# Splitting weight chunks with two GpSimd DMAs and a ScalarE negation instead of a ScalarE cast and a VectorE subtraction

## The chip, the cores and the metric

The kernel runs on one core of a Trainium2 chip. The metric is device time in microseconds (us) of one execution. The engines are PE (TensorE matmul, with PEld for its weight loads), DVE (VectorE), ACT (ScalarE), POOL (GpSimd) and SP (SyncE, which here only issues DMAs). A change of less than 0.2% of the time (1.8 us) counts below as no change, since the three runs of before differ by about that much.

## What is computed

One block of a hybrid network in fp32, for 512 tokens of width 1024:

```python
h = rms_norm(x, norm1_g)
u_x, u_g, q, k, v, g_r, g_a = split(h @ w_in)
y_rnn  = rg_lru(causal_depthwise_conv(u_x), ...) * gelu(u_g)
y_attn = diff_attention(rope(q), rope(k), v, ...)
merged = sigmoid(g_r) * (y_rnn @ w_br_rnn) + sigmoid(g_a) * (y_attn @ w_br_attn)
x  = x + merged @ w_out
x  = x + square(relu(rms_norm(x, norm2_g) @ w_mlp1)) @ w_mlp2
out = rms_norm(x, normf_g)
```

## The kernel before

Every large product is made of three fp32r matmuls, so that fp32 accuracy is kept: both operands are split into a high part rounded to fp32r and a low part that is the remainder, and `mm` adds high x high, high x low and low x high in one PSUM bank (lines 168, 169 and 170).

The weights come in chunks of 128 x 1024 fp32 (512 KB, one block of 128 output columns over all 1024 rows). `chunk_plan` lists them in the order of use: chunks 0 to 7 are V, chunks 8 to 39 are Q, K, U_X and U_G (head by head, with the attention and the recurrent unit beside them), chunks 40 to 71 are the gates and the two branch projections, chunks 72 to 79 are `w_out`. The MLP that follows has its own path (`make_piece`, `hold`) and its own ring.

Two chunks are loaded by one 1 MB DMA on SP into a `raw` tile (two buffers). `emit_chunk` then splits one chunk in two instructions: ACT casts the raw values into the high tile (line 137), DVE subtracts the high tile from the raw values into the low tile (line 138). `wslot` says where they go: tiles `whi` and `wlo` with four buffers each, and for every fifth chunk of the first 40 the tiles `E0` and `E1`. `chunk(c)` emits the split of chunk c+4 (c+3 from about chunk 36 on) before it hands out chunk c, so a split can start when the matmuls of an earlier chunk have released its buffer. A chunk is consumed by `proj`: 24 matmuls of 512 columns. The result in PSUM (tag `mm`, three buffers) is taken away by ACT or DVE; in the merge stage ACT applies the sigmoid to a gate's result and DVE multiplies it with the branch's result.

Each engine runs its own queue in order. A scheduler decides at build time where each instruction stands in its engine's queue; it is not written out by hand. An instruction whose input or buffer isn't ready holds up everything behind it on its engine.

Of the kernel before, what the change touches and what calls it, by code (L numbers as in the profile page):

```python
# [8 lines left out]
F = mybir.dt.float32  # L9
FR = mybir.dt.float32r  # L10
AF = mybir.ActivationFunctionType
ALU = mybir.AluOpType
AX = mybir.AxisListType

P = 128
T = 512
D = 1024
KT = D // P
# [75 lines left out]
class Build:  # L94
# [19 lines left out]

    def emit_chunk(self, c, parts=False):
        nc = self.nc
        if c // 2 not in self.raw:
            raw = self.t("raw", (P, 2, D), bufs=2)
            if c < 4:
                for j in range(4):  # L120
                    nc.sync.dma_start(self.x_in[2 * c + j], self.a["xT"][2 * c + j])
                    nc.sync.dma_start(
                        raw[:, j // 2, (j % 2) * T:(j % 2 + 1) * T],
                        self.a["wts"][c // 2, :, j * T:(j + 1) * T],
                    )
            else:
                nc.sync.dma_start(raw.rearrange("p c f -> p (c f)"), self.a["wts"][c // 2])
            self.raw[c // 2] = raw
        raw = self.raw[c // 2][:, c % 2]
        th, tl, bufs = self.wslot(c)  # L130
        hi = self.t(th, (P, KT, P), FR, bufs=bufs)
        lo = self.t(tl, (P, KT, P), FR, bufs=bufs)
        hf, lf = hi.rearrange("p k m -> p (k m)"), lo.rearrange("p k m -> p (k m)")
        self.split[c] = (hi, lo)

        def part(s):
            nc.scalar.copy(hf[:, s], raw[:, s])  # L137
            nc.vector.tensor_tensor(lf[:, s], raw[:, s], hf[:, s].bitcast(F), op=ALU.subtract)  # L138

        if parts:  # L140
            return part
        part(slice(0, D))
# [827 lines left out]
```

## Time and profile before

| what | us |
|---|---|
| median of three runs | 894.05 (892.45 to 894.46) |
| the profiled execution's own time | 893.03 |
| its span, first to last instruction | 891.2 |
| PE busy in the span | 879.4 |
| DVE busy | 582.0 |
| ACT busy | 474.3 |
| POOL busy | 0.3 |

The span is the stretch that the profile shows; the time of the execution is 1.8 us longer. The engines work side by side, so their busy times don't add up. POOL does five small fills and issues no DMA; all loads and stores are issued by SP.

### The profile page before, as it was taken

The page shows a single profiled execution, that of the slowest core. Times are in us where ns is not written, and L with a number is a line of the kernel's source. Part 1 is how long each engine was busy: PE and PEld are TensorE (multiplying, and loading weights), DVE is VectorE, ACT ScalarE, POOL GpSimd, SP SyncE. Part 2 cuts the span into 40 slices and gives each one's busy share as a digit, 9 for nine tenths or more (in the row PEclk, how much of TensorE's full clock was granted, in tenths as well). Part 3 has the DMA queues.
Part 4 walks back from the last instruction along what each step waited for, and adds up shares of the span by engine and source line. Part 5 has one row for each costly group of instructions (what it writes and reads, how often), then busy time and mean ns, then how long its engine had stood idle before and what let it go on. Part 6 is the DMA issues. An engine that isn't in the chain of part 4 may idle for free.

```text
span 891.2 us, 12316 instructions
## 1 busy us (share of the span) xinstructions
PE 879.4 (99%) x4817; PEld 737.9 (83%) x4817; DVE 582.0 (65%) x995; ACT 474.3 (53%) x857; POOL 0.3 (0%) x5
## 2 busy tenths in 40 slices
PE   9999999999999999999999999999999999999996
PEld 7887778777777788888888889888888888888996
DVE  7777688787887756333333897776666666666633
ACT  7644777957867983322222456655444444445532
POOL 0000000000000000000000000000000000000000
PEclk9999999999999999999999999999999999999998
DMA  8443123132223022222522222232222223322211
GB/s 290 146 143 118 60 71 130 51 121 78 71 105 120 3 95 95 95 94 95 177 95 93 69 102 82 79 112 95 95 96 95 98 101 108 113 92 106 95 49 48
DMA packets 20746, 88.60 MB, mean 99 GB/s; under 512 B 3024, under 2 KB 6352, under 8 KB 11728
## 3 DMA queue, kind: packets, MB, share of 16 engines
q1 hardware_dynamic: 20688, 87.81, 28.7%
q8 instruction: 38, 0.62, 0.3%
q14 instruction: 20, 0.16, 0.1%
HBM read 81.51 MB, written 2.10 MB: 94 GB/s over the span
## 4 chain that ended last, share of the span: by engine, by line
PE 96%; DMA 1%; DVE 1%; ACT 1%; issue 0%; SPq 0%; DVEq 0%; ACTq 0%
PE pmm L242 22%; PE pmm L168 16%; PE pmm L170 15%; PE pmm L169 15%; PE psc L242 15%; PE psc L410 2%; PE psc L498 2%; PE pmm L410 2%; PE pmm L533 2%; PE ptr L521 1%; DMA raw<-wts 1%; PE psc L594 1%; DMA L<-xT 1%; PE ptr L341 0%; PE psc L596 0%
## 5 line engine op out<-in xcount | busy, mean ns | idle before, releaser
L197 ACT CAST whi<-raw 128x512 fp32r<-128x512 f32 (+1 forms) x144 | 87.9, 630 | 134.4 <-PE pmm L242 56.7
L137 ACT CAST whi<-raw 128x1024 fp32r<-128x1024 f32 (+1 forms) x76 | 76.3, 1006 | 134.4 <-PE pmm L169 125.0
L168 PE MATMUL pmm<-X,whi 128*128 128x512 f32 x328 | 132.4, 404 | 0.0
L169 PE MATMUL pmm<-X,whi 128*128 128x512 f32 x328 | 130.1, 397 | 0.0
L170 PE MATMUL pmm<-X,wlo 128*128 128x512 f32 x328 | 130.0, 396 | 0.0
L138 DVE TENSOR_TENSOR wlo<-raw,whi 128x1024 fp32r<-128x1024 f32 (+1 forms) x76 | 88.4, 1164 | 60.2 <-ACT whi L137 59.6
L198 DVE TENSOR_TENSOR wlo<-raw,whi 128x512 fp32r<-128x512 f32 (+1 forms) x144 | 100.0, 703 | 34.2 <-ACT whi L197 31.8
L242 PE MATMUL psc<-X,whi 128*128 128x256 f32 x448 | 84.1, 286 | 0.6 <-DVE up L816 0.2
L168 PEld LDWEIGHTS pmm<-X,whi 128*128 128x128 f32 x328 | 61.7, 188 | 18.1 <-issue 2.6
L170 PEld LDWEIGHTS pmm<-X,wlo 128*128 128x128 f32 x328 | 61.7, 188 | 15.0
L242 PEld LDWEIGHTS psc<-X,whi 128*128 128x128 f32 x448 | 69.0, 188 | 5.9 <-DVE up L816 1.7
L169 PEld LDWEIGHTS pmm<-X,whi 128*128 128x128 f32 x328 | 61.8, 188 | 14.3 <-issue 0.4
L242 PE MATMUL psc<-X,wlo 128*128 128x256 f32 x224 | 60.8, 280 | 0.0
L302 ACT ACTIVATE B<-psc,nb 128x128 f32<-128x128 f32 (+3 forms) x64 | 33.2, 523 | 26.9 <-DVE nb L503 23.9
L242 PE MATMUL psc<-L,whi 128*128 128x256 f32 x224 | 43.7, 291 | 1.7 <-DVE tmp L812 1.7
L302 ACT ACT_TABLE_LOAD x32 | 41.1, 1283 | 1.1 <-DVE nb L503 0.5
L242 PEld LDWEIGHTS psc<-X,wlo 128*128 128x128 f32 x224 | 41.3, 188 | 0.0
L242 PE MATMUL pmm<-R,whi 128*128 128x512 f32 x128 | 41.1, 392 | 0.0
L242 PEld LDWEIGHTS psc<-L,whi 128*128 128x128 f32 x224 | 34.3, 188 | 7.4 <-DVE tmp L812 4.3
L242 PE MATMUL pmm<-Q,whi 128*128 128x512 f32 x128 | 39.7, 391 | 0.0
L242 PE MATMUL pmm<-B,whi 128*128 128x256 f32 (+1 forms) x160 | 37.5, 325 | 0.0
L242 PE MATMUL pmm<-V,whi 128*128 128x512 f32 (+1 forms) x128 | 32.4, 338 | 0.0
(318 smaller groups left out, 1886.3 us busy)
## 6 DMA issues: line engine op xcount, KB each, us to landing
raw<-wts SPq DMA_DIRECT2D x70, 1024.0 KB, 4.8
rot<-B SPq DMA_DIRECT2D x64, 64.0 KB, 2.0
L<-xT SPq DMA_DIRECT2D x8, 256.0 KB, 5.4
raw<-wts SPq DMA_DIRECT2D x8, 256.0 KB, 5.4
E<-xT SPq DMA_DIRECT2D x8, 256.0 KB, 4.8
out<-E SPq DMA_DIRECT2D x6, 256.0 KB, 3.2
tmp<-gates SPq DMA_DIRECT2D x8, 128.0 KB, 4.7
out<-E SPq DMA_DIRECT2D x4, 128.0 KB, 2.8
```

The lines of the kernel that those rows point to most:

```text
L137: nc.scalar.copy(hf[:, s], raw[:, s])
L138: nc.vector.tensor_tensor(lf[:, s], raw[:, s], hf[:, s].bitcast(F), op=ALU.subtract)
L168: nc.tensor.matmul(ps, hi[:, k], xh[k], start=(k == 0), stop=False)
L169: nc.tensor.matmul(ps, hi[:, k], xl[k], start=False, stop=False)
L170: nc.tensor.matmul(ps, lo[:, k], xh[k], start=False, stop=(k == KT - 1))
L197: self.nc.scalar.copy(hi, src)
L198: self.nc.vector.tensor_tensor(lo, src, hi.bitcast(F), op=ALU.subtract)
L242: nc.tensor.matmul(out, l[:, k], r, start=((first if clear is None else clear) and k == 0 and g == 0), stop=(last and k == 3 and g == 2), ...
L302: ins = A.activation(*args, **kw).ins
L410: TE.matmul(pvs[half][i], xs[q][:, i * P:(i + 1) * P], (hv, lv)[wi][:, q % 2], start=(q == 0 and n == 0), stop=(q == KT - 1 and n == 2))
L498: TE.matmul(sc[:, m, :n], l[rows, 0, i * P:n], r[rows, 1, :n], start=(g == 0), stop=(g == 2))
L533: TE.matmul(po[:, i], pdT[:, j], v[j][:, h * P:(h + 1) * P], start=(j == 0), stop=(j == i))
```

## The change

For every chunk from 8 on, `emit_chunk` leaves SP's raw load, ACT's cast and DVE's subtraction out. The high tile is written by a DMA that GpSimd issues straight from the weights in HBM and that casts fp32 to fp32r. ACT then writes the negated high part into the low tile, and a second GpSimd DMA adds the raw weights from HBM onto that tile. Chunks 0 to 7 and the MLP weights stay as they were.

```diff
     def emit_chunk(self, c, parts=False):
         nc = self.nc
+        if c >= 8:
+
+            src = self.a["wts"][c // 2, :, c % 2 * D:(c % 2 + 1) * D]
+            th, tl, bufs = self.wslot(c)
+            hi = self.t(th, (P, KT, P), FR, bufs=bufs)
+            lo = self.t(tl, (P, KT, P), FR, bufs=bufs)
+            hf, lf = hi.rearrange("p k m -> p (k m)"), lo.rearrange("p k m -> p (k m)")
+            nc.gpsimd.dma_start(hf, src)
+            nc.scalar.mul(lf, hf.bitcast(F), -1.0)
+            nc.gpsimd.dma_start(lf, src, accum_op=ALU.add)
+            self.split[c] = (hi, lo)
+            return
         if c // 2 not in self.raw:
```

This is POOL's queue in the middle of the merge stage after the change; before, POOL's queue holds no DMA anywhere. L124 is the casting DMA of a chunk and L126 its accumulating DMA; `whi_666` and `wlo_667` are the two tiles of one chunk, `whi_669` and `wlo_670` those of the next, and so on.

```order
L124 DMA whi_666_3258<-wts 128x1024
L126 DMA wlo_667_3259<-wts 128x1024
L124 DMA whi_669_3289<-wts 128x1024
L126 DMA wlo_670_3290<-wts 128x1024
L124 DMA whi_674_3325<-wts 128x1024
L126 DMA wlo_675_3326<-wts 128x1024
L124 DMA whi_677_3356<-wts 128x1024
L124 DMA whi_681_3388<-wts 128x1024
L126 DMA wlo_678_3357<-wts 128x1024
L126 DMA wlo_682_3389<-wts 128x1024
```

The first three chunks stand one by one: the cast of a chunk is queued behind the accumulation of the chunk before. The last two stand as a pair, with both casts ahead of both accumulations. From chunk 48 to chunk 53 six chunks stand one by one; then seven times a pair and a single; then a single, a pair and two singles. The four chunks 44 to 47 ahead of them overlap. Of chunks 8 to 43, 24 stand one by one and 12 as six pairs.

ACT's queue at the same place before the change. L302 is the sigmoid of a gate's result in PSUM, L137 the cast of a chunk, L353 the high part of the merged result:

```order
L302 ACTIVATE tmp_687_3258<-pmm_690_3263 128x512
L137 CAST whi_697_3326<-raw_691_3289 128x1024
L353 CAST R0_695_3322<-tmp_687_3258 128x512
L137 CAST whi_701_3358<-raw_700_3356 128x1024
L302 ACTIVATE up2_696_3325<-pmm_699_3330 128x512
L137 CAST whi_705_3389<-raw_700_3356 128x1024
L137 CAST whi_709_3421<-raw_708_3419 128x1024
L302 ACTIVATE tmp_704_3388<-pmm_707_3393 128x512
```

And after it (the same three lines are now L314, L125 and L365; the buffer numbers are others):

```order
L125 ACTIVATE wlo_670_3290<-whi_669_3289 128x1024
L365 CAST R0_672_3321<-tmp_665_3257 128x512
L125 ACTIVATE wlo_675_3326<-whi_674_3325 128x1024
L314 ACTIVATE up2_673_3324<-pmm_676_3330 128x512
L125 ACTIVATE wlo_678_3357<-whi_677_3356 128x1024
L125 ACTIVATE wlo_682_3389<-whi_681_3388 128x1024
L314 ACTIVATE tmp_680_3387<-pmm_683_3393 128x512
```

In this piece each cast has become a negation at the same place to within one instruction. The negation waits for a DMA where the cast waited for a buffer that PE releases, and the sigmoids and casts behind it wait with it.

## Rows read from the trace of the kernel before

**Rows 1.** The page, parts 1 and 2: busy time of engines, tenths in 40 slices.

```profile
PE 879.4 (99%) x4817; PEld 737.9 (83%) x4817; DVE 582.0 (65%) x995; ACT 474.3 (53%) x857; POOL 0.3 (0%) x5
...
PE   9999999999999999999999999999999999999996
```

**Rows 2.** Stretches: length, busy time of engines, PE clock, DMA share, GB/s.

```profile
29.00:52.70 23.70, 23.70 (x112) 19.43 (x110) 18.02 (x40) 13.08 (x20) 0.00 (x0) 1.00 0.38 130
52.70:321.70 269.00, 268.96 (x1312) 209.81 (x1310) 207.98 (x382) 192.54 (x376) 0.00 (x0) 1.00 0.26 86
321.70:529.00 207.30, 207.30 (x925) 168.48 (x925) 102.33 (x138) 73.95 (x114) 0.00 (x0) 1.00 0.29 102
529.00:825.00 296.00, 293.72 (x1914) 262.69 (x1913) 204.29 (x344) 149.15 (x273) 0.00 (x0) 1.00 0.28 97
```

**Rows 3.** The page, part 4: the chain that ended last, by engine.

```profile
PE 96%; DMA 1%; DVE 1%; ACT 1%; issue 0%; SPq 0%; DVEq 0%; ACTq 0%
```

**Rows 4.** ACT's timeline: start, length, what, idle time before and its releaser.

```profile
400.10 1.05 ACT L137 CAST whi<-raw 128x1024 fp32r<-128x1024 f32 x1 [4.27 <-PE pmm L169]
401.06 0.59 ACT L302 ACTIVATE tmp<-pmm 128x512 f32<-128x512 f32 x1
405.62 1.05 ACT L137 CAST whi<-raw 128x1024 fp32r<-128x1024 f32 x1 [3.97 <-PE pmm L169]
...
422.51 1.05 ACT L137 CAST whi<-raw 128x1024 fp32r<-128x1024 f32 x1 [4.56 <-PE pmm L169]
```

**Rows 5.** Groups by line and shape: count, busy us, mean ns, idle before.

```profile
L138 DVE TENSOR_TENSOR wlo<-raw,whi 128x1024 fp32r<-128x1024 f32 x68 | 82.9, 1221 | 59.9 <-ACT whi L137 59.3
L197 ACT CAST whi<-raw 128x512 fp32r<-128x512 f32 x140 | 83.9, 618 | 132.4 <-PE pmm L242 56.7 <-PE psc L242 48.1 <-DVE raw L214 15.9
L319 ACT ACTIVATE X<-L,small 128x512 fp32r<-128x512 f32 x15 | 10.6, 717 | 5.5 <-PE pmm L410 4.0 <-DMA L<-xT 1.5
```

**Rows 6.** DMA: the queue's total, then issues with size and us to landing.

```profile
q1 hardware_dynamic: 20688, 87.81, 28.7%
...
raw<-wts SPq DMA_DIRECT2D x70, 1024.0 KB, 4.8
rot<-B SPq DMA_DIRECT2D x64, 64.0 KB, 2.0
```

**Rows 7.** SP's timeline: one issue of a 1 MB load.

```profile
161.82 0.33 SPq L127 DMA_DIRECT2D raw<-wts  x1
```

**Rows 8.** ACT's line 137 from 52.7 to 321.7 us: what ended its waits.

```profile
  PE pmm L169: 26.6, 10
```

## The prediction

> **What bounds the kernel now.** I read the engines' busy shares first, then the stretches, then the chain. PE is busy 879.4 of 891.2 us [rows 1], and the chain that ended last is PE for 96% [rows 3]. The stretches sharpen this [rows 2]. The chunks that the change touches run from 52.7 to 529 us, and PE's idle time there is 0.04 us. DVE is busy 208 of 269 us in the first part and 102 of 207 in the second, so it has room; ACT has 76 us of room in the first part and 133 in the second. Removing work from DVE or ACT can therefore give back next to nothing. What counts is whether a chunk's two tiles still arrive before PE wants them.
>
> In the merge stage PE takes 5.60 us a chunk: four successive casts span 400.10 to 422.51 us [rows 4]. Chunks 44 to 79 take 207.3/36 = 5.8 us on average and chunks 8 to 43 take 269/36 = 7.5 us, the attention's matmuls included [rows 2]. ACT's casts wait for PE to release a buffer, up to 4.56 us, and start as soon as it does [rows 4]. The lead is large: with four buffers a released one is needed again three chunks later, 3 x 5.60 = 16.8 us, and cast plus subtraction fill it in 1.05 + 1.22 us [rows 4, 5].
>
> **The change part by part.** Removed: 72 subtractions of 1.22 us on DVE (88 us [rows 5]), worth nothing in time, since PE's work covers them; 36 loads of 1 MB on SP, hidden as well. ACT's 72 casts of 1.05 us become 72 negations. A scaled copy on half the columns takes 0.717 against 0.618 us for a cast [rows 5], so I take 1.15 us; the 7 us in all lie in ACT's room. The transfers change from 72 x 512 KB read once to read twice, and the second one also reads and rewrites the low tile.
>
> What costs is the new chain of a chunk: POOL issues the cast, it lands, ACT negates, POOL issues the accumulation, it lands. POOL runs in order, so where chunks stand one by one, the next cast can't be issued before this chunk's negation. That gives POOL a cycle time of its own. None of these DMAs is in the trace, so I bound them.
>
> Transfer: 64 KB land in 2.0 us and 1 MB in 4.8 [rows 6], a line of 1.8 us plus 2.9 us per MB. 512 KB alone lands in 3.3 us; that is the lower end. The accumulation moves its bytes over at least two reads, so I count it as 1 MB. It is issued right ahead of the next cast and the two share the 16 DMA engines; sharing evenly, the cast has landed when 1 MB has moved, 4.7 us, and the accumulation when 1.5 MB has, 6.2 us. The upper end is half that speed, for casting or adding on the way: 7.6 and 10.6 us. I take 4.7 and 6.2, since the nearest row, the 1 MB load, moves as much through the same engines.
>
> Issue on POOL: SP spends 0.33 us on a load [rows 7]; that is the lower end. The upper end is 2.0 us, the whole of the shortest DMA [rows 6]. I take 1.0 us. ACT: 1.15 us for the negation and 0.25 for the semaphores and a short queue, 1.4 us; the sigmoid ahead of it would add 0.59 [rows 4].
>
> The cast then costs 1.0 + 4.7 = 5.7 us to landing. A single takes 5.7 + 1.4 + 1.0 = 8.1 us of POOL's cycle; a pair, whose second negation follows the first, 5.7 + 2 x 1.4 + 1.0 = 9.5 us. The whole chain of one chunk is 5.7 + 1.4 + 1.0 + 6.2 = 14.3 us of the 16.8, so 2.5 us of slack.
>
> Chunks 8 to 43: 24 singles and six pairs need 24 x 8.1 + 6 x 9.5 = 251 us, and PE takes 269, so weights keep up on the whole. ACT pays instead: ten casts waited for a buffer there, 26.6 us [rows 8], and those ten will wait for the cast's landing as well, 10 x 5.7 = 57 us more. ACT's room is 269 - 192.5 - 26.6 = 50 us beyond these waits [rows 2, 8]. What is behind it on ACT is the softmax and the recurrent unit's sigmoids, for which PE waits. I charge the excess, **7 us**; ends 0 (the buffered PSUM tiles cover it) and 57.
>
> Chunks 44 to 79: the first four overlap and cost nothing. Six singles lag by 6 x (8.1 - 5.6) = 15.0 us. A pair and a single take 17.6 us against PE's 16.8, seven times 0.8 = 5.6. The last five take 3 x 8.1 + 9.5 = 33.8 against 28.0, 5.8. Together 26.4, less the slack of 2.5: **24 us**. Behind the late negations stand the sigmoids and with them DVE's multiplications; three PSUM buffers give these two chunks of time, so they add nothing of their own.
>
> Sum: 893.0 (the profiled execution, 1 us under the median of the runs shown) + 24 + 7 = **924 us**.
>
> A rule speaks against this result. The Trainium skill, "DMA: Bandwidth & Descriptors", section "Anatomy of one DMA — SWDGE (gpsimd) path", gives a DMA from GpSimd about 2.0 us fixed plus its bytes at 436 GB/s; for 512 KB that is an estimate of 3.2 us, near the line's 3.3 us, and with it alone the sum would stay at 893 (the first rival's place). The line from SP's loads agrees with it to 0.1 us; no row of before shows a DMA from GpSimd.
>
> **The rivals.** *Hidden after all: 893.* At the lower ends the cast lands in 0.33 + 3.3 = 3.6 us, a single cycles in 3.6 + 1.4 + 0.33 = 5.3 us, under PE's 5.6, the chain takes 3.6 + 1.4 + 0.33 + 3.3 = 8.6 of 16.8 us, and ACT's ten waits grow by 36 us, under its 50. For it speaks that the DMA engines are loaded to 28.7% only [rows 6]; against it, that every term must stay near its lower end, since six singles in a row, with the 8.2 us of slack that this chain leaves, allow a cycle of 7.0 us at most. This is the case that isn't slower.
>
> *Slow transfers: about 1,063.* At half speed the cast lands in 8.6 us; a single is 11.0, a pair 12.4. Chunks 44 to 79 lag by 6 x 5.4 + 7 x 6.6 + 17.4 = 96 us, and by 4.8 more since the chain is 21.6 us long, over the 16.8; chunks 8 to 43 need 24 x 11.0 + 6 x 12.4 = 338 us against 269, 69 more. 893 + 101 + 69 = 1,063. The engines themselves speak for it: 87.81 MB took 28.7% of 891.2 us [rows 6], 1.53 us per 512 KB; a cast and a double-sized accumulation at half speed would take 9.2 us of them a chunk, more than PE's 5.6 or 7.5. At full speed they take 4.6, which fits. If only POOL's issue is at its upper 2.0 us, a single takes 10.1 us and a pair 11.5: 311 us against 269 in the first part, 74 us of lag in the second, about 1,010.
>
> *POOL held up by DVE: about 950.* If POOL's descriptor work has to wait while DVE holds a port, an issue waits on average half of a 1.22 us operation in the share of time that DVE is busy: 0.77 in the first part, 0.49 in the second [rows 2, 5], 0.5 and 0.3 us an issue, two issues a chunk. Singles become 9.1 and 8.7 us. The first part then needs 24 x 9.1 + 6 x 10.5 = 281 us, 12 over; in the second the lags grow by 14. The Trainium skill, "SBUF — State Buffer", section "SBUF: two separate sides", has this lock for DVE's two-port modes; no run here shows it yet.
>
> *Faster: about 891.* The raw tiles come free earlier for the MLP; PE's idle time from 529 to 825 us is 2.3 us [rows 2], and all of it would have to vanish.
>
> **How the numbers follow.** My own case, weights late by a few us in the merge stage: 0.40, with its own range of 897 to 960. Held up by DVE, inside that range: 0.05. Hidden: 0.20. Slow transfers or a slow issue, 960 to 1,100: 0.27; beyond: 0.05. Faster: 0.03. The range of 892 to 1,070 leaves out the faster case and the upper half of the slow one with what lies beyond, about 0.2. The bound for no change is 0.2%, or 1.8 us. Faster 0.03, same 0.20, slower 0.77.
>
> **What the profile would show.** Right: PE idle from some 350 us on, ended by the DMA into `wlo`, some 24 us in all and almost none before 321 us; POOL's queue alternating with a period near 8 us for singles; cast DMAs landing in 4 to 6 us, accumulations in 5 to 7; ACT's idle time before line 125 ended by the cast DMA; DVE's busy time near 494 us. Wrong: no PE idle time there (hidden); DMA engines near full with landings of 8 us and more (slow transfers); long issues on POOL (slow issue). What would make it wrong most easily is the price of an accumulating DMA, the term that rests on the farthest row, or ACT's waits stopping PE in the attention stage, where I charge only 7 us.

## The result and the profile after

The changed kernel takes 1000.1 us (median of three runs, 998.0 to 1002.68) against 894.05: 1.119 times the time before (95% interval 1.117 to 1.121). The forecast was 924 us in a range of 892 to 1,070. The direction and the range held; the move was 106 us where 30 were expected.

The page after, parts 1 to 3, answers to [rows 1, 6]: busy times, the tenths of PE and of its granted clock in 40 slices, and the two DMA queues (q0 is GpSimd's).

```profile
PE 907.4 (91%) x4817; PEld 752.9 (75%) x4817; DVE 499.3 (50%) x923; ACT 472.8 (47%) x857; POOL 103.3 (10%) x149
...
PE   8996798799799599899888988899999999999996
...
PEclk9997899799799799999999999999999999999998
...
q0 software_dynamic: 20736, 75.51, 33.2%
q1 hardware_dynamic: 15504, 50.06, 14.9%
```

PE has gaps from the fourth slice on, through both stages, and its busy time has grown by 28 us for the same 4817 instructions, with a granted clock of 0.7 to 0.8 in the slices in which PE is busy for 5 to 7 tenths. DVE has lost 83 us of work, and it bought nothing.

The two stages as stretches, with the columns of [rows 2]:

```profile
55.00:384.90 329.90, 284.71 (x1312) 220.07 (x1310) 165.81 (x330) 192.65 (x376) 50.52 (x71) 0.92 0.56 127
384.90:632.00 247.10, 217.44 (x927) 171.94 (x926) 60.89 (x101) 73.29 (x112) 47.53 (x66) 0.97 0.66 155
```

The attention stage has grown from 269.0 to 329.9 us, the merge stage from 207.3 to 247.1. The span grew by 109.6: 2.3 ahead of the stages, 60.9, 39.8, and 6.6 behind them. Within the attention stage PE's busy time rose by 15.7 us and its idle time to 45.2; within the merge stage by 10.1 and to 29.7. PE's waits in the attention stage, 55.0 to 384.9 us (who waits, for whom: us in all, times, the longest):

```profile
PE psc L606 <- ACT L L314: 28.6, 4, 11.4
PE psc L507 <- DVE B L489: 8.8, 1, 8.8
PE psc L606 <- ACT gwh L601: 7.4, 2, 3.8
```

And in the merge stage:

```profile
PE pmm L182 <- DMA wlo<-wts: 21.1, 11, 3.0
PE ptr L574 <- DVE V L332: 5.5, 2, 3.9
PE pmm L180 <- ACT Q L365: 2.9, 1, 2.9
PE pmm L181 <- DVE Q L366: 0.2, 1, 0.2
```

These rows add up to the idle time, 44.8 of 45.2 and 29.7 of 29.7 us. In the merge stage PE waits for weights, as forecast. In the attention stage no row names a weight: PE waits for the recurrent unit's gates (lines 601 to 608) and once for the rotated Q and K (line 489), all from ACT and DVE. ACT's own waits for casts in that stage are 22, with 87.9 us (L125 is the negation; `E` stands for the tiles `E0` and `E1`):

```profile
ACT wlo L125 <- DMA whi<-wts: 72.5, 18, 8.7
ACT E L125 <- DMA E<-wts: 15.4, 4, 6.9
```

The waits of POOL, ACT and DVE over the whole span, in this order:

```profile
POOL wlo L126 <- ACT wlo L125: 337.1, 58, 11.7
POOL whi L124 <- PE pmm L182: 60.3, 19, 7.9
...
ACT wlo L125 <- DMA whi<-wts: 185.9, 39, 9.2
...
DVE B L487 <- DMA rot<-B: 62.5, 13, 16.8
```

The DMA issues with their size and median us to landing:

```profile
whi<-wts POOLq DMA_DIRECT2D x65, 512.0 KB, 6.9
wlo<-wts POOLq DMA_DIRECT2D x65, 512.0 KB, 5.5
...
rot<-B SPq DMA_DIRECT2D x64, 64.0 KB, 5.5
```

POOL stands 337 us behind negations and ACT 186 us behind casts (the tiles `E0` and `E1` add 33 and 17). The prediction hadn't looked at the last row: the 64 KB loads of the rotary embedding, issued by SP and untouched by the diff, take 5.5 us instead of 2.0 [rows 6], and DVE waits 62.5 us for them (3.9 before). Not all of this is the landing: the loads start from ACT's copies of Q and K (line 478), and these stand behind negations as well. Two such copies at 64.06 and 74.33 us, for example, stand behind negations that had waited 5.22 and 8.73 us for their casts; DVE then waits 16.77 and 6.79 us for the loads.

POOL's timeline in the merge stage shows its cycle:

```profile
434.34 0.86 POOL L126 DMA_DIRECT2D wlo<-wts  x1 [6.63 <-ACT wlo L125]
434.88 0.89 POOL L124 DMA_DIRECT2D whi<-wts  x1
443.10 0.86 POOL L126 DMA_DIRECT2D wlo<-wts  x1 [7.33 <-ACT wlo L125]
443.64 1.43 POOL L124 DMA_DIRECT2D whi<-wts  x2
451.43 0.89 POOL L126 DMA_DIRECT2D wlo<-wts  x1 [6.36 <-ACT wlo L125]
452.74 0.87 POOL L126 DMA_DIRECT2D wlo<-wts  x1 [0.41 <-ACT wlo L125]
453.54 0.62 POOL L124 DMA_DIRECT2D whi<-wts  x1
462.16 0.87 POOL L126 DMA_DIRECT2D wlo<-wts  x1 [8.00 <-ACT wlo L125]
```

A single takes 8.76 us (434.34 to 443.10), a pair and a single 19.06 (443.10 to 462.16). PE can use a chunk every 5.60.

How a late cast reaches PE in the attention stage is seen near 250 us and near 340 us, first on ACT's timeline:

```profile
250.05 1.06 ACT L125 ACTIVATE wlo<-whi 128x1024 fp32r<-128x1024 f32 x1 [3.56 <-DMA whi<-wts]
251.01 0.39 ACT L601 CAST gwh<-tmp 128x256 fp32r<-128x256 f32 x1
...
336.91 1.06 ACT L125 ACTIVATE wlo<-whi 128x1024 fp32r<-128x1024 f32 x1 [7.70 <-DMA whi<-wts]
```

And on PE's:

```profile
251.45 0.80 PE L606 MATMUL psc<-L,gwh 128*128 128x512 f32 x1 [3.68 <-ACT gwh L601]
252.05 0.63 PE L607 MATMUL psc<-R,gwh 128*128 128x512 f32 x1
...
257.55 0.39 PE L180 MATMUL pmm<-X,whi 128*128 128x512 f32 x1
...
342.05 0.80 PE L606 MATMUL psc<-L,gwh 128*128 128x512 f32 x1 [11.38 <-ACT L L314]
```

ACT stands 3.56 us in front of a negation whose cast hasn't landed. The gate's cast, whose input SP had loaded from 225.28 us on, is next in ACT's queue, and PE waits 3.68 us for it. The last two lines are the longest wait of the stage: ACT stands 7.70 us in front of a negation, the softmax and a gate's sigmoid (line 314) come behind it, and PE waits 11.38 us. Of PE's seven waits in this stage five, with 30.8 us, have such a stand of ACT at a negation (3.3 to 7.7 us) right ahead. The other two, 8.8 us until 86.27 and 5.3 us until 111.82, follow waits of DVE for rotary loads. After the wait near 250 us the same 512 columns take 0.63 us, later 0.39: the granted clock is 0.50 from 251.40 to 256.70, the lower of the two levels (1.2 of 2.4 GHz). Such stretches are where the added busy time comes from: the mean granted clock is 0.92 in the attention stage and 0.97 in the merge stage, against 1.00 before, so a wait here costs more than its length.

### The profile page after: what moved, and what is told of

Its sections match the earlier page's. It is cut to its first block, busy times and chain, and to the rows that moved or that the text cites. A ratio compares the mean times of both kernels' runs of the same rounds, so it can differ in the third digit from the quotient of the medians.

```text
span 1000.8 us, 12512 instructions
## 1 busy us (share of the span) xinstructions
PE 907.4 (91%) x4817; PEld 752.9 (75%) x4817; DVE 499.3 (50%) x923; ACT 472.8 (47%) x857; POOL 103.3 (10%) x149
## 3 DMA queue, kind: packets, MB, share of 16 engines
q0 software_dynamic: 20736, 75.51, 33.2%
HBM read 119.26 MB, written 2.10 MB: 121 GB/s over the span
## 4 chain that ended last, share of the span: by engine, by line
PE 55%; issue 20%; DMA 14%; POOL 4%; ACT 3%; DVE 3%; SPq 0%; POOLq 0%; DVEq 0%; ACTq 0%
PE pmm L254 19%; PE psc L254 13%; DMA whi<-wts 8%; PE pmm L182 5%; PE pmm L180 5%; PE pmm L181 5%; DMA wlo<-wts 2%; POOL whi L124 2%; PE pmm L422 2%; PE psc L422 2%; POOL wlo L126 1%; DMA raw<-wts 1%; PE psc L510 1%; ACT wlo L125 1%; DMA E<-wts 1%
## 5 line engine op out<-in xcount | busy, mean ns | idle before, releaser
L125 ACT ACTIVATE wlo<-whi 128x1024 fp32r<-128x1024 f32 x65 | 68.8, 1058 | 229.4 <-DMA whi<-wts 185.9
L209 ACT CAST whi<-raw 128x512 fp32r<-128x512 f32 (+1 forms) x144 | 87.9, 630 | 126.3 <-PE pmm L254 56.9
L182 PE MATMUL pmm<-X,wlo 128*128 128x512 f32 x328 | 133.4, 407 | 7.5 <-DMA wlo<-wts 7.5
L180 PE MATMUL pmm<-X,whi 128*128 128x512 f32 x328 | 135.7, 414 | 0.0
L181 PE MATMUL pmm<-X,whi 128*128 128x512 f32 x328 | 132.6, 404 | 0.0
L126 POOL DMA_DIRECT2D wlo<-wts x65 | 56.6, 870 | 376.6 <-ACT wlo L125 337.1
L182 PEld LDWEIGHTS pmm<-X,wlo 128*128 128x128 f32 x328 | 63.9, 195 | 24.8 <-DMA wlo<-wts 9.2
L180 PEld LDWEIGHTS pmm<-X,whi 128*128 128x128 f32 x328 | 63.8, 194 | 18.8 <-issue 2.3
L181 PEld LDWEIGHTS pmm<-X,whi 128*128 128x128 f32 x328 | 63.7, 194 | 14.6
L124 POOL DMA_DIRECT2D whi<-wts x65 | 47.4, 760 | 98.6 <-PE pmm L182 60.3
L705 DVE TENSOR_TENSOR tmp<-pmm,tmp 128x512 f32<-128x512 f32 x8 | 5.5, 691 | 76.2 <-PE pmm L182 51.0
L606 PE MATMUL psc<-L,gwh 128*128 128x512 f32 x16 | 10.3, 643 | 36.4 <-ACT L L314 28.6
L487 DVE TENSOR_TENSOR B<-B,up 128x512 f32<-128x512 f32 x16 | 11.0, 691 | 62.5 <-DMA rot<-B 62.5
```

Source lines behind the costliest of these rows:

```text
L124: nc.gpsimd.dma_start(hf, src)
L125: nc.scalar.mul(lf, hf.bitcast(F), -1.0)
L126: nc.gpsimd.dma_start(lf, src, accum_op=ALU.add)
L180: nc.tensor.matmul(ps, hi[:, k], xh[k], start=(k == 0), stop=False)
L181: nc.tensor.matmul(ps, hi[:, k], xl[k], start=False, stop=False)
L182: nc.tensor.matmul(ps, lo[:, k], xh[k], start=False, stop=(k == KT - 1))
```

## The experiments

Three theories. **A**: ACT's queue, held up at negations behind a cast's landing, is the cause. **B**: POOL's cycle is, since its in-order queue puts cast, negation and accumulation of successive chunks one behind the other. **C**: the crowded DMA engines are, since they make the casts and the rotary loads late. This table has the stages of the profiled executions and the times in us. The ratios are to runs of before on the same chip, made beside each kernel. The attention stage runs from the first projection with chunk 8 to the first projection with chunk 44, a branch projection; the merge stage runs from there to the end of `w_out`.

| kernel | attention stage | merge stage | median | ratio to before (95%) |
|---|---|---|---|---|
| before | 269.0 | 207.4 | 894.05 | |
| after | 329.9 | 247.1 | 1000.1 | 1.117 to 1.121 |
| e1 negation on POOL | 360.5 | 355.5 | 1133.6 | 1.267 to 1.271 |
| e2 no accumulation | 280.3 | 209.9 | 906.6 | 1.011 to 1.018 |
| e3 high part only | 288.5 | 208.8 | 921.1 | 1.029 to 1.033 |
| e4 merge stage only | 268.9 | 245.3 | 938.8 | 1.048 to 1.054 |
| e5 cast one chunk ahead | 290.9 | 211.3 | 922.3 | 1.031 to 1.036 |
| e6 low part only | 292.1 | 208.2 | 917.9 | 1.023 to 1.030 |
| e7 plain loads, twice | 273.0 | 207.5 | 898.7 | 1.003 to 1.007 |
| e8 negation on DVE | 335.8 | 263.2 | 1026.2 | 1.145 to 1.155 |
| e9 = e5 without rotary loads | 274.7 | 211.8 | 905.0 | 1.011 to 1.014 |
| e10 = after without rotary loads | 312.8 | 243.7 | 973.2 | 1.084 to 1.090 |
| e11 = before without rotary loads | 270.3 | 207.6 | 896.5 | 1.002 to 1.004 |
| e12 = e4 with the cast one ahead | 269.0 | 209.6 | 898.4 | 1.003 to 1.006 |

**e1 and e8: the negation on another engine.** On POOL, ACT has no part in the split; on DVE, a faster engine does it.

```diff
-            nc.scalar.mul(lf, hf.bitcast(F), -1.0)
+            nc.gpsimd.tensor_scalar(lf, hf.bitcast(F), -1.0, None, op0=ALU.mult)   # e1
+            nc.vector.tensor_scalar(lf, hf.bitcast(F), -1.0, None, op0=ALU.mult)   # e8
```

> The negation moves from ACT's queue to POOL's own queue; both DMAs stay. Theory A (ACT is held up: in the attention stage ACT's softmax, sigmoids and gate casts stand behind negations that wait for the cast to land, and PE waits for them): the attention stage, 330 us in the changed kernel and 269 before, comes back to under 290 us, and PE's waits for ACT at the recurrent gates (36 us) go to under 8. Theory B (POOL's cycle: weights are late because cast, negation and accumulation follow each other on POOL): the merge stage (247 us against 207) stays above 240 and may grow, since a cycle of 6.9 + negation + 0.9 us remains, and the attention stage comes back little, to over 315. Theory C (the DMA engines are crowded, so the rotary loads and the casts land late): nothing comes back in the attention stage, rotary loads still land in about 5.5 us.

Measured 1133.6 us. POOL's timeline:

```profile
427.63 2.77 POOL L125 TENSOR_SCALAR wlo<-whi 128x1024 fp32r<-128x1024 f32 x1 [5.67 <-issue]
430.69 0.91 POOL L126 DMA_DIRECT2D wlo<-wts  x1 [0.30 <-POOL wlo L125]
431.29 0.88 POOL L124 DMA_DIRECT2D whi<-wts  x1
438.40 2.77 POOL L125 TENSOR_SCALAR wlo<-whi 128x1024 fp32r<-128x1024 f32 x1 [6.23 <-issue]
```

PE's waits over the span:

```profile
PE pmm L182 <- DMA wlo<-wts: 141.1, 46, 8.3
...
PE psc L606 <- ACT gwh L601: 2.6, 2, 2.2
```

The negation takes 2.77 us on POOL against 1.06 on ACT, and the cycle is 10.77 us here; the stages take 360.5/36 = 10.0 and 355.5/36 = 9.9 us a chunk. ACT stands behind no cast, the gates wait 2.6 us, and PE now waits for the weights themselves: here POOL's cycle alone sets the time. A as the only cause falls.

> The negation moves from ACT's queue to DVE's; both DMAs stay on POOL and are interleaved much as in the changed kernel. Theory A: ACT is free, its waits for casts and PE's 36 us of waits for ACT at the recurrent gates go; DVE now stands behind the casts, so part comes back as PE's waits for DVE; attention stage 285 to 315 us. Theory B: no better than the changed kernel, merge stage 240 us or more; if the negation takes 0.6 us on DVE instead of 1.06, POOL's cycle falls by that and each stage by some 10 to 15 us. Total by A about 965, by B 975 to 1000.

Measured 1026.2 us. The negation is faster (0.695 us), but DVE now stands 244.1 us behind the casts, ACT 111.9 us behind DVE's softmax maxima (line 515), and PE 40.6 us at the gates: the wait is carried by another engine. The time lies above both forecasts, and the merge stage grew by 16 us where B expected it to shrink. The edit changed more than the engine: the scheduler now gives POOL four pairs from chunk 48 on, where the changed kernel has eight. A single takes 8.0 us (437.31 to 453.27 us for two), less than the changed kernel's 8.6, but with fewer pairs the 31 steps between the accumulations of these chunks take 7.6 us on average instead of 7.1.

**e4: the change from chunk 44 on** (`if c >= 44:`).

> The change is made for chunks 44 to 79 alone (branch projections, gates of the second half, w_out); chunks 8 to 43 are split as before. If the two stages add up: 894 + 39 for the merge stage + up to 7 behind it = 933 to 941 us, with an attention stage of 269 us. If the merge stage is late only because the attention stage hands over without lead: under 925. By the prediction's term of 24 us: 918.

The merge stage takes 245.3 us without a change ahead of it and 247.1 with one, and the attention stage is that of before. So the stages' costs add up. POOL stands 193.9 us behind negations there, and PE 19.9 us behind the accumulation.

**e2 and e3: no accumulation.** e2 leaves the accumulating DMA out, so that the low part is the negated high part; e3 keeps the raw loads and DVE's subtraction, and makes only the high part with GpSimd's cast.

```diff
-            nc.gpsimd.dma_start(lf, src, accum_op=ALU.add)   # e2
...
+        if c >= 8:   # e3, ahead of DVE's subtraction; no cast on ACT
+            nc.gpsimd.dma_start(hf, self.a["wts"][c // 2, :, c % 2 * D:(c % 2 + 1) * D])
```

> The accumulating DMA is left out, so the low part is the negated high part; cast and negation stay where they are. Theory A: ACT still stands behind the casts, so the attention stage stays above 300 us; PE still waits for ACT at the gates. Theory B: POOL no longer waits for ACT, so casts run ahead of need and land by the time ACT comes to them; both stages come back to within 8 us of before (269 and 207), total about 900. Theory C: the traffic falls to what it was before, rotary loads land in about 2 to 3 us, the attention stage comes back to under 290 us, and the merge stage too.

> Only the high part is changed: cast by a GpSimd DMA; the raw chunk is loaded on SP as before and DVE subtracts as before. ACT does nothing for these chunks, POOL waits for no engine but PE's release of a buffer. The bytes read are those of the changed kernel, without the accumulation's second pass. Theory A and theory B: back near before, 893 to 905 us, unless DVE, which now stands behind the cast's landing, takes ACT's place (then PE waits for DVE in the attention stage, 905 to 930). Theory C: rotary loads still land in 4 us or more and the attention stage stays above 300 us, total over 920.

Both lose nearly all of the cost in the merge stage and keep 11 and 20 us in the attention stage. For e2 that is less than A expected and, in the attention stage, more than the 8 us of B. The landing of a cast without accumulations is 3.8 us in e2 and 4.1 in e3, and rotary loads take 3.7 us in both; these are e3's rows:

```profile
whi<-wts POOLq DMA_DIRECT2D x65, 512.0 KB, 4.1
rot<-B SPq DMA_DIRECT2D x64, 64.0 KB, 3.7
```

ACT's waits in e2, over the whole span:

```profile
ACT wlo L125 <- DMA whi<-wts: 124.2, 52, 5.8
```

ACT still waits 124.2 us for casts, and the time rises by only 13 us: ACT's waiting by itself is cheap when POOL isn't in the loop. In e3 DVE stands 91.7 us behind casts, and the time lies in the 905 to 930 us expected for that case.

**e6: the low part only.** The raw loads on SP and ACT's cast stay; ACT also negates, and GpSimd adds.

```diff
+            if c >= 8:   # in place of DVE's subtraction
+                nc.scalar.mul(lf, hf.bitcast(F), -1.0)
+                nc.gpsimd.dma_start(lf, self.a["wts"][c // 2, :, c % 2 * D:(c % 2 + 1) * D], accum_op=ALU.add)
+                return
```

> The other half of the change alone: the raw chunk is loaded on SP and cast on ACT as before; ACT negates as well, and a GpSimd DMA accumulates the raw weights onto the low part. No cast DMA, so ACT stands behind no DMA from POOL and POOL has one DMA a chunk. The bytes of the accumulation stay. Theory A and B: no loss from either, so 894 to 905 us (ACT's 76 us more of work have room). Theory C: rotary loads land in over 3.5 us and the attention stage is above 285 us, total over 912.

```profile
wlo<-wts POOLq DMA_DIRECT2D x65, 512.0 KB, 6.2
rot<-B SPq DMA_DIRECT2D x64, 64.0 KB, 5.1
```

This gives the price that no row of before had: an accumulation lands in 6.2 us and takes 23.3% of 917.4 us for 72 of them, 2.97 us of the 16 DMA engines each, twice the 1.53 of a plain 512 KB. ACT stands behind no GpSimd DMA, and still 23 us are lost in the attention stage, with rotary loads at 5.1 us and DVE 51.6 us behind them. That is what C expected; A and B had expected no loss.

**e7: bytes alone.** Each raw pair from chunk 8 on is loaded a second time, by a plain GpSimd DMA.

```diff
+                if c >= 8:
+                    nc.gpsimd.dma_start(raw.rearrange("p c f -> p (c f)"), self.a["wts"][c // 2])
```

> The kernel before, with each 1 MB raw load of chunks 8 to 79 followed by a second, plain load of the same bytes into the same tile, issued on POOL: 36 DMAs that nothing else waits for than the cast and subtraction of those chunks, which have lead. The bytes read are those of the changed kernel, without the accumulation's pass. Theory A and B: 893 to 897 us. Theory C: the rotary loads land in over 3 us, DVE waits for them by 20 us or more, and the time is over 900.

```profile
rot<-B SPq DMA_DIRECT2D x64, 64.0 KB, 2.0
```

The same 119.26 MB are read from HBM as after the change, for some 5 us. The rotary loads stay at 2.0 us. So bytes alone are not the cause. These loads differ from the casts and accumulations in more than being plain: they are 1 MB each and move 37.75 MB in 5184 packets, where the casts of e2 and the accumulations of e6 are 512 KB each and take 10368 packets for as many bytes. Which of these differences matters wasn't tried.

**e5: the cast one chunk ahead.** Negation and accumulation of a chunk are issued after the next chunk's cast, so POOL always has one cast on its way. The lines left out of `finish` keep the accumulation behind that cast (`after`) in POOL's queue.

```diff
+    def finish(self, after):
+        lf, hf, src = self.late.pop(0)
+        self.nc.scalar.mul(lf, hf.bitcast(F), -1.0)
+        add = self.nc.gpsimd.dma_start(lf, src, accum_op=ALU.add).ins
...
-            nc.gpsimd.dma_start(hf, src)
-            nc.scalar.mul(lf, hf.bitcast(F), -1.0)
-            nc.gpsimd.dma_start(lf, src, accum_op=ALU.add)
+            cast = nc.gpsimd.dma_start(hf, src).ins
...
+            self.late.append((lf, hf, src))
+            if len(self.late) > 1:
+                self.finish(cast)
+            if c == self.mlp0 - 1:
+                self.finish(None)
```

> Same instructions as the changed kernel, but on POOL each cast stands ahead of the accumulation of the chunk before, all the way through, so that a cast no longer waits for the negation before it. ACT still negates, and both DMAs still move the same bytes (4.6 us of the 16 DMA engines a chunk, under PE's 5.6 and 7.5). Theory B (POOL's cycle of 6.9 + 1.1 + 0.9 us is what makes weights and ACT late): the merge stage comes back from 247 to 207 to 215 us and the attention stage from 330 to under 290, total 895 to 925. Theory A (ACT is held up at the negations whatever POOL's order): merge stage back, attention stage still above 310 us. Theory C (crowded DMA engines): both stay, over 960 in all, with landings above 7 us.

Measured 922.3 us: 78 of the 106 us are gone, with every DMA and negation still there. POOL's timeline in the merge stage:

```profile
403.81 0.55 POOL L136 DMA_DIRECT2D whi<-wts  x1 [4.17 <-PE pmm L197]
404.35 0.90 POOL L119 DMA_DIRECT2D wlo<-wts  x1
409.37 0.56 POOL L136 DMA_DIRECT2D whi<-wts  x1 [4.12 <-PE pmm L197]
...
415.00 0.55 POOL L136 DMA_DIRECT2D whi<-wts  x1 [3.35 <-PE pmm L197]
```

The landings:

```profile
whi<-wts POOLq DMA_DIRECT2D x65, 512.0 KB, 5.1
wlo<-wts POOLq DMA_DIRECT2D x65, 512.0 KB, 7.5
...
rot<-B SPq DMA_DIRECT2D x64, 64.0 KB, 6.0
```

POOL now runs at PE's 5.6 us and waits for PE's buffers, and no matmul waits for a weight. That is theory B, with a reserve: the edit moves the negation on ACT by a chunk too, so it doesn't part POOL's order from ACT's. e1 and e2 bear on that from either side: with ACT out of the split and a cycle of 10.77 us the loss grows, and with POOL free of ACT's negations at most 13 us are lost while ACT stands behind the casts for 124. What it leaves is 21.9 us in the attention stage, with rotary loads at 6.0 us.

**e9, e10, e11: the rotary loads left out.** The small loads are removed from e5, after and before; DVE's three operations stay.

```diff
-        for j in range(4):
-            s = j * 32
-            o = s + 32 if j % 2 == 0 else s - 32
-            nc.sync.dma_start(rots[n][o:o + 32], qk[s:s + 32, n])
...
+            V.tensor_tensor(rots[n], qk[:, n], sinr, op=ALU.mult)
             V.tensor_tensor(qk[:, n], qk[:, n], cosr, op=ALU.mult)
-            V.tensor_tensor(rots[n], rots[n], sinr, op=ALU.mult)
```

> The version with the cast one chunk ahead, and without the sixteen rotary loads' 64 small DMAs: the rotated half is made from the same rows instead (the rotation across rows is left out, DVE does the same three operations). With these loads that version has an attention stage of 290.9 us against 269.0, PE waits at the gates for ACT 11.7 us, and DVE waits 50.6 us for the rotary loads, which land in 6.0 us instead of 2.0. Theory C (the crowded DMA engines reach PE through the late rotary loads: DVE late, then ACT, then the gates): attention stage 270 to 276 us, no wait at the gates, total 898 to 904. Rival (the late loads are covered; the residual of 22 us comes from the order of ACT's queue or from weights): attention stage 286 to 292 us, total 915 to 922.

> The changed kernel without the rotary loads, in the same way (the rotation across rows is left out). Its attention stage is 329.9 us. Theory B (POOL's cycle sets this stage by itself; rotary loads are late beside it): 320 to 330 us, total 990 to 1000. Theory B plus C as parts that add up: 330 less some 20, 305 to 312 us, total 975 to 982. The merge stage stays at 247 in both.

> Control: the kernel before without the rotary loads (the rotation across rows is left out). Its rotary loads land in 2.0 us and DVE waits 3.9 us for them in all, so every theory expects no change: attention stage 268 to 269.5 us, total 892 to 895. A gain here would have to be taken off the gain of the other two.

The control e11 gained nothing and was 2.6 us slower than before. e9's attention stage fell by 16.2 us to 274.7, e10's by 17.1 to 312.8. From e10 to e9, the cast one ahead takes 38.1 us off this stage; from after to e5 it took 39.0. The two parts add up in both orders, as B plus C said, if not to the microsecond (312.8 us against 305 to 312 expected for e10, 905.0 against 898 to 904 for e9). In the medians e10 gains 26.9 us over after, more than its stage shows; its stages are those of an execution of 981.1 us, 8 us above its median. e9's attention stage as a stretch:

```profile
52.90:327.60 274.70, 270.11 (x1312) 209.54 (x1310) 165.65 (x331) 192.67 (x377) 50.52 (x71) 1.00 0.66 137
```

The granted clock is back at 1.00 and PE's busy time at 270; the gates wait 4.0 us for ACT there (11.7 in e5), while ACT stands 154.6 us behind casts over the span.

**e12: the merge stage alone, and the cast one chunk ahead.** The change for chunks 44 to 79 only, one cast ahead.

> The change for chunks 44 to 79 alone, with the cast one chunk ahead; the complete computation. From the stages measured apart: attention stage 269, merge stage 211 (one ahead) and 2 to 7 us in the rest: 897 to 903. If the merge stage's 38 us in the version for this stage alone came from something other than POOL's cycle, some of it stays: 915 to 935.

898.4 us, as the stages measured apart had it: the merge stage is 2.2 us longer than before, and POOL's remaining wait behind negations, 33.5 us, reaches nobody. It is the best complete version of the idea that was tried, and still slower than before.

## Why the prediction was right in direction and wrong in size

- **What bounds the kernel**: right. The 83 us taken from DVE gave nothing back in any run.
- **The merge term, 24 us, measured 39.8**: the mechanism held, PE's wait for the low tile alone being 21.1 us. Two sizes were off. The cast lands 7.2 us after its issue there (4.7 + 1.0 taken), because the step that let cast and accumulation *share evenly* was wrong: a cast lands in 3.8 us without accumulations (e2), in 6.9 behind one, and in 5.1 ahead of one (e5), where the accumulation goes from 5.5 to 7.5. By these medians they land in the order of issue. An issue costs POOL less than the 1.0 us taken: 0.54 us from an accumulation to the next cast. So a single became 8.6 us on average (six of them from 391.66 to 443.10) instead of 8.1, a pair and a single 20.05 (seven from 443.10 to 583.46) instead of 17.6. With these, the same sum gives 6 x 3.0 + 7 x 3.25 + 9.8 for the last five (37.84 us from 583.46 to 621.30, less 28.0), some 50 us of lag, part of which the lead of the weights hides. The second size was the clock: 10.1 us of the 39.8 are PE's busy time after gaps, which the sum didn't have.
- **The attention term, 7 us with ends of 0 and 57, measured 60.9**: this is the step that failed. It netted ten ACT waits of 57 us against 50 us of average room on ACT, and let POOL's 251 us of need pass under PE's 269. ACT's waits came out near the size that this gives with the old ones (87.9 us in 22 waits, against 26.6 + 57 = 84 in ten). What failed is the netting: the room lay elsewhere in the stage, while gates and softmax stood right behind the late negations, and PE lost 30.8 us there. POOL's need didn't pass under PE's time either: POOL waited 74 us there for PE to release buffers, in the same stage in which PE waited 45 us for ACT and DVE. The queues wait for each other in turn, and time that one spends waiting can't be saved up for later. 39 of the 61 us go when the cast is issued one chunk ahead (e5).
- **Not in the sum at all: the rotary loads**, 16 to 17 us of the same stage (e9, e10); PE's two waits behind them in after are 14.1 us. The text looked at what stood behind the new DMAs on POOL and ACT, and not at SP's small loads, which share the DMA engines. Some 6 us of this stage remain in e9 beyond before's 269.0.
- **The rivals**: the transfers weren't slow as such. Queue q0 was busy 33.2% of 1000.8 us, 4.61 us of engine time a chunk, against 4.6 forecast for full speed and 9.2 for half. POOL held up by DVE isn't needed: the issues last 0.53 to 0.95 us in all runs but for four of 1.0 to 1.2 us (one in e6, three in e8), and after's casts are issued in 0.73 us on average both where DVE is busy meanwhile and where it is idle. The Trainium skill, "SBUF — State Buffer", section "SBUF: two separate sides", has that lock; nothing in these runs shows it. The hidden case is nearest to what e12 reaches.
- **The rule cited against the forecast**: a lone cast showed 3.8 us in e2, the chain 6.9. The 3.2 us by the Trainium skill, "DMA: Bandwidth & Descriptors", section "Anatomy of one DMA — SWDGE (gpsimd) path", is near the first and far from the second. A rule that would have helped stands in the Trainium skill, on the same page, "DMA: Bandwidth & Descriptors", section "Two DMAs through the same engine are not ordered": within one queue of a DMA engine descriptors start in order. The landings of after and e5 agree with it. With it, an estimate from e2 and e6 for a cast issued 0.54 us behind an accumulation is 2.97 - 0.54 + 3.8 = 6.2 us; 6.9 was measured, so the order gives most of the delay and not all.
- **DVE's busy time** of 499.3 us was forecast at 494.

What stays open: why e3 keeps 20 us and e6 23 in the attention stage. Rotary loads are late in both (3.7 and 5.1 us), and e5's share of this is shown by e9, but neither was run without them. Nor was it settled which property of the casting and accumulating DMAs (the cast or addition, the size, the number of packets) delays SP's small loads. The 6.6 us behind the two stages weren't traced; e5 and e12 have 2 to 3 of them left.

## What to carry to other kernels

A chain of DMA, engine, DMA on one in-order queue has a cycle time of its own; compare it with the consumer's pace, and issue the next item's first DMA ahead of this item's last. Don't net an engine's waits against its average room: look at who stands behind each waiting instruction, and list the small loads of other queues that share the DMA engines. Here PE had no idle time, so the work taken off DVE, which had room, gave nothing back. And read the queue again after each edit: where a scheduler places the instructions, an edit can change their order too, as in e8.

## What the hardware showed unexpectedly

- A 512 KB accumulating DMA into SBUF from HBM took 2.97 us of the 16 DMA engines, a casting one 1.74 (13.8% of 908.0 us for 72, e2), a plain one 1.48 (11.9% of 896.8 us for 36 loads of 1 MB, e7).
- 64 KB loads issued by SP landed in 2.0 us beside plain GpSimd loads (DMA share of the attention stage 0.46, e7), in 3.7 beside casts (0.29 and 0.46, e2 and e3), and in 5.1 to 6.0 beside accumulations (0.57 and 0.66, e6 and e5). The share alone doesn't tell them apart.
- The negation of a 128x1024 tile took 0.695 us on DVE, 1.06 on ACT and 2.81 on POOL (means).
- A PE wait of 3.68 us was followed by 5.3 us at a granted clock of 0.50.
